# Second block of a two-block decoder trunk: x for the operands' sums comes in whole rows into the raw weights' places, the norm's diagonals are made ahead of their matmuls, and the weight sums begin with the first output units

## Chip, cores, metric

One Trainium2 chip, one core. The metric is the device time of one execution in microseconds (us); the time given for a kernel is the median of its runs. One execution is also taken by the hardware profiler; its records are the profile that is quoted here.

## What is computed

One layer of a decoder trunk on x of 2048 tokens by 1024 features, all in float32:

```
h = rmsnorm(x, mix_norm_g)
q, k, v, g, u = split(h @ w_in)                    # 4 x 512 columns for retention, 512 for pooling
y_ret  = silu(g) * head_rmsnorm(retention(rope(q), rope(k), v))
y_pool = pool_mixer(u)                             # trailing windows 2, 4, 8, 16
x = x + concat(y_ret, y_pool) @ w_out
x = x + cross_attn(rmsnorm(x), mem)                # 4 heads, 256 memory tokens
x = x + (silu(gate) * val) @ w_down                # gate, val: causal conv of width 3 over rmsnorm(x) @ w_up
out = rmsnorm(x)
```

## The kernel before

Features lie on the 128 partitions, tokens along the free dimension. The tokens are worked in **two blocks** of T = 1024 (b = 0, 1); in each, a stage works on halves of SUB = 512 tokens. A float32 product is made of three passes (`passes`, L266 to L268): every operand is split into a high half (fp32r, ScalarE) and a low half (the rest, VectorE), and high x high, high x low, low x high are summed in a PSUM bank (`mm`, five of them, beside two `aux` and one single). So each weight tile costs one ScalarE and one VectorE operation per 512 columns before TensorE can use it (`split`, `pairs`, and `high`, `low` of `Member`, L1092 and L242).

**Places.** SBUF is handed out by hand. `raws` are the places of unsplit weights: R (three of 128x1024) and two tiles S; `prs` are the places of split pairs, Q (three). `TT` is an arena of ten places T of 512 columns for everything short-lived. `Z` has eight places of 1024 columns. A place that is taken again makes its next writer wait for its last reader.

**Order.** The program is recorded in Python order, and a scheduler then sets each engine's order. Generators are advanced between products: `behind[0]` (work that must come soon: retention, norms), `under[0]` (the weight sums), and inside a stage one of its own. The order of an engine's queue, its SP queue of DMA issues included, is fixed once it is built; each waits for the instruction in front of it.

**Weight sums** (`weight_sums`). The second block's input projections and all of the gated MLP are done in seven products of half-size blocks instead of eight. They need sums of weight blocks, which GpSimd's DMA queue makes in DRAM: copies of 128x512 (L990) and accumulating transfers (L987). There are 42 jobs (8 for the head projections, 22 up, 12 down) of four steps each. One more job is begun at each step; a step starts with a halo copy on ScalarE (L1005) and one on GpSimd (L1006), behind which GpSimd issues up to eight transfers for the up to four jobs alive. `spacing[0]` calls of the generator lie between two steps. It is called after each quarter of a unit (while `slow[0]` holds, which is until the first block's output projection, after every second one), after each tile of the attention (L956; in the first block from its sixth on), after each quarter of the second block's values and after each of its 56 head products. In the products with VWd it is paused.

**The second block's start**, on which the change works. The last products of the first block (with VWd, `unit`) run beside the loading of the second block's x (`load_x`) and of the values' weights wv (`opening`, four loads into R and S). Then:

- `norms` (a generator in `behind[0]`) makes the factors of the norm by `rows_norm` (sums over partitions by TensorE, L347, then some 14 small VectorE operations) and spreads them over the partitions by `spread`: for each half a diagonal matrix per high and low part (VectorE, into a Q place), each followed at once by a matmul of `ones` with it (L371), and an evacuation (L376).
- `values` makes v: eight token tiles in four rounds of two banks, two half-rounds each; between them `between` advances `quarter_sums`, and the weight sums.
- `quarter_sums` makes the operands of the seven products from x, in four groups j. A group takes four T places, loads a quarter of 128x512 into each (L1540), and computes with ScalarE and VectorE the split of (x11 - x12) g1 into t1 (L1549, L1550), d3 and d4 into Z (L1555, L1559), and the negated split of x11 g1 + d3 into t2 (`negated`, L1562).
- `head_projections` turns `raws` into seven places of 512 columns (five in R, two in one S) and S0 into a fourth pair place, loads weights (`fetch`, L1086) and splits them up to four products ahead. Its first steps are `turned_sums` (d3 into t3 and d4 into the operand X) and `scaled_tables` (rope tables times the norm). It evacuates with L1659. One bank is summed on over several products, with an evacuation between them.

In the second attention (`attention`) ScalarE splits tables Md that SP loads (L905) among the first tiles' work, and the transposes of finished tiles (L920) stand among TensorE's products.

Of the kernel before, what the change touches and what calls it, by code (L numbers as in the profile page):

```python
# [8 lines left out]
F32 = mybir.dt.float32  # L9
F32R = mybir.dt.float32r  # L10
# [5 lines left out]
P = 128  # L16
# [120 lines left out]
def trunk(ctx, tc, xT, memT, pos, w_qkgu, w_v, wkv, wqT, wo, wout_r, wout_p, poolT, w_up, w_dn, vecs, consts, outT):  # L137
# [178 lines left out]
    def units(weights, rhs, evacs, order, at):  # L316
# [3 lines left out]
        for h in range(2):  # L320
            for hs, evac, banks in zip(weights, evacs, ps):
                if callable(hs[h]):
                    hs[h] = hs[h]()
                for s in range(NS):
# [4 lines left out]
                    quarter[0] += 1  # L329
                    if not slow[0] or quarter[0] % 2:  # L330
                        next(under[0], None)
# [23 lines left out]
    def spread(y, outs, keep=True, late=False):  # L355
# [8 lines left out]
        for out in outs:  # L364
# [12 lines left out]
            at += n  # L377
        return last

    def squares(k, src, s_ap, eng=dve):  # L380
# [316 lines left out]

    def values(rn, wp, step=lambda: None):
        v = Z.take(4)
        v4 = v.f.rearrange("p (h c d) -> p h c d", h=HEADS, c=KT)  # L700
# [191 lines left out]
    def attention(sums, beside, pace):  # L892
# [39 lines left out]
        for i in range(2 * KT):  # L932
# [631 lines left out]

    def head_projections(b, v, rb, tabs, t1, t2, z3, z4):

# [13 lines left out]
        def turned_sums():  # L1580
            for j in range(KT // 2):
                split(z3.f[:, j * SUB : (j + 1) * SUB], *fourth(t3, j))
                yield
            z3.free()
            for j in range(KT // 2):
                negated(z4.f[:, j * SUB : (j + 1) * SUB], *xpair(j, 1))
                yield
            z4.free()

# [285 lines left out]
    for b in range(NB):  # L1875
# [19 lines left out]
        else:  # L1895
            t1, t2 = (B.arenas[0].take(4) for _ in range(2))
            z3, z4 = Z.take(2), Z.take(2)
            more_sums = quarter_sums(b, t1, t2, z3, z4)

# [4 lines left out]

            v = values(lambda: normed[0], wv, between)
            for _ in more_sums:
# [4 lines left out]
            for i in range(2):  # L1911
                sp.dma_start(tabs[i].f[:, :SUB], rope_d[i])
            mix = head_projections(b, v, rb, tabs, t1, t2, z3, z4)
        for r in rb:
            r.free()
        slow[0], spacing[0] = False, (8, 4)[b]

# [43 lines left out]
        prob, behind[0] = attention(xs, beside, b + 1)  # L1961
        spacing[0] = 4
        for _ in beside:
# [56 lines left out]
        if b + 1 < NB:  # L2020
# [4 lines left out]
            def norms(xs, nxt, normed, own):  # L2025
# [134 lines left out]
```

## Time and profile before

| | us |
|---|---|
| median of 3 runs | 2492.06 |
| lowest, highest | 2489.83, 2493.7 |
| the profiled execution | 2488.75 |
| its span, first to last instruction | 2487.0 |
| mean granted TensorE clock | 0.991 |
| TensorE busy | 2424.5 |
| VectorE busy | 1731.5 |
| ScalarE busy | 1288.9 |
| GpSimd busy | 319.2 |

Names: PE is TensorE, DVE VectorE, ACT ScalarE, POOL GpSimd, SP SyncE, which issues most DMAs (SPq its queue). In a row of the order of time stand start, duration, engine, line, operation, out<-in, shape, and in brackets the idle time of the engine ahead of it and what ended it. In the chain of work stand start, duration and what was worked on or waited for. In the table of DMA issues stand out<-in, queue, count, KB each and the median time from issue to landing. L242, L250, L258 and L261 are helpers (two-input operations, fused three-input operations, and the two forms of a high half), so there the tiles tell what is meant.

### The profile page before, as it was taken

How to read it: one execution, taken by the hardware profiler on the slowest of the kernel's cores; microseconds unless marked ns; L12 is line 12 of the kernel's file. 1: busy time of each engine (PE TensorE's matmuls, PEld its weight loads, DVE VectorE, ACT ScalarE, POOL GpSimd, SP SyncE). 2: the span in 40 equal slices, each digit the busy share in tenths (PEclk: the TensorE clock that was granted, in tenths of full speed). 3: DMA queues.
4: the chain of work that ended last, by engine and by line, in shares of the span. 5: the costliest groups of instructions: out<-in, count | busy, mean ns of one | idle time of the engine just before them, and what ended most of it. 6: DMA issues, size and time to landing. Idle time of an engine off the chain costs nothing.

```text
span 2487.0 us, 33308 instructions
## 1 busy us (share of the span) xinstructions
PE 2424.5 (97%) x11294; PEld 2021.6 (81%) x11294; DVE 1731.5 (70%) x2921; ACT 1288.9 (52%) x2348; POOL 319.2 (13%) x485
## 2 busy tenths in 40 slices
PE   6999999999989999999999999999999999999997
PEld 6888888888777787788888888888888888888886
DVE  8645676565666666575588776797667688867875
ACT  6333423443334553334555555665555677666663
POOL 1002022031243424200000000020000000000000
PEclk9999999999999999999999999999999999999998
DMA  8245677677696959847458665665556468768951
GB/s 285 65 136 171 190 181 206 205 169 229 193 239 185 237 141 308 226 166 266 153 178 279 209 190 172 206 222 169 165 158 215 133 223 301 247 187 274 350 170 68
DMA packets 264315, 501.56 MB, mean 202 GB/s; under 512 B 28880, under 2 KB 57680, under 8 KB 264144
## 3 DMA queue, kind: packets, MB, share of 16 engines
q1 hardware_dynamic: 202256, 385.11, 47.6%
q0 software_dynamic: 37376, 86.00, 15.0%
q10 hardware_dynamic: 24512, 28.32, 3.3%
q8 instruction: 89, 1.46, 0.2%
q14 instruction: 82, 0.67, 0.1%
HBM read 398.13 MB, written 187.17 MB: 235 GB/s over the span
## 4 chain that ended last, share of the span: by engine, by line
PE 89%; DMA 4%; DVE 4%; ACT 2%; issue 1%; SPq 0%; POOLq 0%; POOL 0%; DVEq 0%; ACTq 0%
PE mm L266 28%; PE mm L267 28%; PE mm L268 28%; DMA T<-xT 1%; DVE T L242 1%; DMA T<-Xd 1%; PE aux L266 1%; PE aux L782 1%; PE aux L267 1%; PE aux L268 1%; PE aux L798 1%; PE aux L771 1%; DMA R<-Md 1%; PE aux L800 1%; DVE Z L242 0%
## 5 line engine op out<-in xcount | busy, mean ns | idle before, releaser
L266 PE MATMUL mm<-G,Q 128*128 128x512 f32 (+1 forms) x1745 | 675.6, 388 | 29.2 <-ACT Q L258 11.0
L268 PE MATMUL mm<-G,Q 128*128 128x512 f32 (+1 forms) x1745 | 671.0, 386 | 6.3 <-DVE Q L242 6.2
L267 PE MATMUL mm<-G,Q 128*128 128x512 f32 (+1 forms) x1617 | 622.1, 385 | 0.0
L267 PE MATMUL mm<-G,E 128*128 128x512 f32 x1084 | 421.6, 389 | 0.0
L266 PE MATMUL mm<-G,E 128*128 128x512 f32 x1084 | 420.0, 389 | 0.0
L268 PE MATMUL mm<-G,E 128*128 128x512 f32 x1084 | 419.2, 389 | 0.0
L266 PEld LDWEIGHTS mm<-G,Q 128*128 128x128 f32 x1745 | 332.8, 191 | 96.1 <-ACT Q L258 12.1
L268 PEld LDWEIGHTS mm<-G,Q 128*128 128x128 f32 x1745 | 332.1, 190 | 72.2 <-DVE Q L242 9.1
L267 PEld LDWEIGHTS mm<-G,Q 128*128 128x128 f32 x1617 | 308.9, 191 | 56.7
L242 DVE TENSOR_TENSOR Z<-Z,mm 128x512 f32<-128x512 f32 x296 | 202.1, 684 | 104.7 <-PE mm L268 104.4
L250 DVE SCALAR_TENSOR_TENSOR Z<-Z,vecs 128x1024 f32<-128x1024 f32 x176 | 224.8, 1281 | 50.4 <-ACT Z L1155 46.9
L268 PEld LDWEIGHTS mm<-G,E 128*128 128x128 f32 x1084 | 203.5, 188 | 42.4
L267 PEld LDWEIGHTS mm<-G,E 128*128 128x128 f32 x1084 | 203.5, 188 | 42.3
L266 PEld LDWEIGHTS mm<-G,E 128*128 128x128 f32 x1084 | 203.5, 188 | 42.0
L242 DVE TENSOR_TENSOR T<-T 128x512 f32<-128x512 f32 (+3 forms) x217 | 148.9, 689 | 39.5 <-ACT T L387 15.6
L1092 ACT ACTIVATE E<-R 128x512 fp32r<-128x512 f32 (+1 forms) x165 | 101.5, 615 | 143.0 <-PE mm L267 132.6
L242 DVE TENSOR_TENSOR G<-T,G 128x512 fp32r<-128x512 f32 (+1 forms) x185 | 122.6, 676 | 41.8 <-ACT G L1041 31.4
L242 DVE TENSOR_TENSOR Q<-R,Q 128x512 fp32r<-128x512 f32 x149 | 103.6, 698 | 65.1 <-ACT Q L258 46.0
L1092 ACT ACTIVATE Q<-R 128x512 fp32r<-128x512 f32 (+1 forms) x153 | 94.4, 617 | 88.0 <-PE mm L267 77.3
L1041 ACT ACTIVATE G<-T 128x512 fp32r<-128x512 f32 x160 | 97.7, 624 | 56.4 <-DMA T<-Hd 26.5
L1155 ACT ACTIVATE Z<-Z,vecs 128x1024 f32<-128x1024 f32 x88 | 109.2, 1242 | 33.3 <-DVE Z L242 32.4
L1092 ACT ACTIVATE E<-S 128x512 fp32r<-128x512 f32 (+1 forms) x107 | 65.8, 616 | 105.7 <-PE mm L267 104.4
(322 smaller groups left out, 3814.8 us busy)
## 6 DMA issues: line engine op xcount, KB each, us to landing
T<-Gd SPq DMA_DIRECT2D x173, 256.0 KB, 4.5
Ud<-w_up POOLq DMA_DIRECT2D x132, 256.0 KB, 9.2
Gd<-Z SPq DMA_DIRECT2D x110, 256.0 KB, 2.8
R<-Ud SPq DMA_DIRECT2D x106, 256.0 KB, 2.7
R<-w_up SPq DMA_DIRECT2D x80, 256.0 KB, 3.1
S<-Ud SPq DMA_DIRECT2D x70, 256.0 KB, 2.8
T<-xT SPq DMA_DIRECT2D x64, 256.0 KB, 4.9
Gd<-T SPq DMA_DIRECT2D x56, 256.0 KB, 3.3
```

Of the source, the lines that this page charges most:

```text
L242: return eng.tensor_tensor(out=out, in0=a, in1=b, op=op)
L250: dve.scalar_tensor_tensor(out=out, in0=a, scalar=s, in1=b, op0=op0, op1=op1)
L266: pe.matmul(ps, lh, rh, start=start, stop=False, skip_group_check=more)
L267: pe.matmul(ps, lh, rl, start=False, stop=False, skip_group_check=more)
L268: latest[0] = pe.matmul(ps, ll, rh, start=False, stop=stop, skip_group_check=more)
L771: pe.matmul(col(sc, c), self.ch(k, c), self.ch(q, c), start=True, stop=True)
L782: pe.matmul(col(self.kv, c), col(self.kn.f, c), self.ch(v, c, h * T), start=True, stop=True)
L798: pe.matmul(col(y, c), col(self.pr.f, c), self.ch(v, c, h * T), start=True, stop=self.cur[c] is None)
L800: pe.matmul(col(y, c), self.ch(q, c), self.cur[c], start=False, stop=True)
L1041: act.activation(hi, x, AF.Copy)
L1092: act.activation(p2[:, 0, :w], self.raw[i].f[:, :w], AF.Copy)
L1155: act.activation(self.c[g].f, a[:, 2:], AF.Identity, bias=cb[:, f : f + 1], scale=cw[2][:, f : f + 1])
```

## The change

Four things. **x in rows:** `quarter_sums` takes places of `raws` instead of T places: for a group two loads of 128x1024, x rows j and j + 4 of the block, each in a whole place of R or S; the first two groups are asked for ahead of the values, and group j + 2 when group j is done. One T place is left for a scratch. d3 and d4 lie in one Z region of four places that is taken with the values' region. **Diagonals ahead:** `spread_steps` makes all four diagonals (two pair places), waits two turns of the generator, and then issues the four matmuls and two evacuations. **Weight sums:** none in the first block's heads and pools; one call per quarter from the output units on with a spacing of 4 instead of 8; in the first attention from the third tile on instead of the sixth; a spacing of 3 instead of 4 in the second block's values and heads.

The diff's core (line numbers of after.py run 22 to 33 higher behind `spread_steps`):

```diff
@@ units
-                    if not slow[0] or quarter[0] % 2:
+                    if not slow[0]:
                         next(under[0], None)
@@ new, behind spread
+    def spread_steps(y, outs):
+        yh = smp.tile([P, 8], F32R, tag="yh", name=nm("yh"), bufs=1)[:, : y.shape[1]]
+        yl = small(y.shape[1])
+        dve.tensor_copy(yh, y)
+        tt(dve, yl, y, yh.bitcast(F32), ALU.subtract)
+        n, ds = SUB // P, []
+        for s in range(len(outs)):
+            ds.append(prs.take())
+            for i, v in enumerate((yh.bitcast(F32), yl)):
+                di = ds[s].r[:, i * SUB : (i + 1) * SUB]
+                tt(dve, di.rearrange("p (a b) -> p a b", a=n), ident..., bcast(v[:, s * n : (s + 1) * n], P), ALU.mult)
+        yield
+        yield
+        for out, d in zip(outs, ds):
+            ps = aux()
+            with tc.issue_after(latest[0].ins):
+                for i in range(2):
+                    pe.matmul(ps, ones, d.r[:, i * SUB : (i + 1) * SUB], start=i == 0, stop=i == 1)
+            d.free()
+            act.activation(out, ps, AF.Copy)
@@ attention
-            if pace > 1 or i > 4:
+            if pace > 1 or i > 1:
                 next(under[0], None)
@@ quarter_sums
+    def part_of(z, i, j):
+        at = (j // 2) * 2 * T + i * T + (j % 2) * SUB
+        return z.f[:, at : at + SUB]
+
-    def quarter_sums(b, t1, t2, z3, z4):
+    def quarter_sums(b, t1, t2, z):
+        def load(j):
+            out = []
+            for k in (j, j + 4):
+                out.append(new_raw())
+                sp.dma_start(out[-1], xT[k * P : (k + 1) * P, b * T : (b + 1) * T])
+            return [r[:, h * SUB : (h + 1) * SUB] for r in out for h in range(2)]
+
+        ahead = [load(0), load(1)]
+        yield
         for j in range(KT // 2):
-            x = [TT.take() for _ in range(4)]
-            for i, r in enumerate(x):
-                k, at = j + 4 * (i // 2), b * T + i % 2 * SUB
-                sp.dma_start(r.f[:, :SUB], xT[k * P : (k + 1) * P, at : at + SUB])
-            x11, x12, x21, x22 = (r.f[:, :SUB] for r in x)
-            d3, d4 = (z.f[:, j * SUB : (j + 1) * SUB] for z in (z3, z4))
+            x11, x12, x21, x22 = ahead.pop(0)
+            d3, d4 = part_of(z, 0, j), part_of(z, 1, j)
             g1, g2 = mixg[:, j : j + 1], mixg[:, j + 4 : j + 5]
-            yield
-            yield
-            x.append(TT.take())
-            t = x[4].f[:, :SUB]
+            r = TT.take()
+            t = r.f[:, :SUB]
             act.activation(t, x12, AF.Identity, scale=g1)
...
             stt(d4, x21, g2, x11, ALU.mult, ALU.subtract)
-            for r in x:
-                r.free()
+            r.free()
+            if j + 2 < KT // 2:
+                ahead.append(load(j + 2))
             yield
@@ trunk, second block
-            z3, z4 = Z.take(2), Z.take(2)
-            more_sums = quarter_sums(b, t1, t2, z3, z4)
+            v, z = Z.take(4), Z.take(4)
+            more_sums = quarter_sums(b, t1, t2, z)
+            next(more_sums)
...
-        slow[0], spacing[0] = False, (8, 4)[b]
+        slow[0], spacing[0] = False, (4, 4)[b]
...
         prob, behind[0] = attention(xs, beside, b + 1)
-        spacing[0] = 4
+        spacing[0] = 3
@@ norms
-                with tc.issue_after(latest[0].ins):
-                    normed[2] = spread(normed[0], [r.f[:, :SUB] for r in normed[1]], late=True)
-                yield
+                yield from spread_steps(normed[0], [r.f[:, :SUB] for r in normed[1]])
                 yield
```

What it does to the built order, at three places. The queue of **SP** at the second block's start, of before (T<-xT behind L1540 are the quarters for the sums, Ad and w_qkgu the head weights, R and S_79 the raw places):

```order
L1086 DMA R<-Ad 128x512
L1086 DMA R<-w_qkgu 128x512
L1540 DMA T<-xT 128x512
L1086 DMA R<-Ad 128x512
L1540 DMA T<-xT 128x512
L1086 DMA R<-Ad 128x512
L1086 DMA R<-w_qkgu 128x512 x2
L1086 DMA R<-Ad 128x512
L1540 DMA T<-xT 128x512
L1086 DMA R<-w_qkgu 128x512
L1540 DMA T<-xT 128x512 x10
L1086 DMA R<-Ad 128x512
```

And now (L1566 loads the x rows, L1108 the head weights; the first x row stands a few places earlier):

```order
L1566 DMA R<-xT 128x1024 x2
L1566 DMA S_78<-xT 128x1024
L1566 DMA R<-xT 128x1024
L1945 DMA T<-rope_d 128x512 x2
L1566 DMA R<-xT 128x1024
L1566 DMA S_79<-xT 128x1024
L1108 DMA R<-Ad 128x512
L1566 DMA R<-xT 128x1024
L1108 DMA S_79<-w_qkgu 128x512
L1108 DMA R<-Ad 128x512
L1108 DMA R<-w_qkgu 128x512
```

Eight of the head weights' loads stood ahead of nearly all of x; now none does, and x is through after eight loads.

The queue of **VectorE** around the norm's diagonals (Q<-consts,yh and Q<-consts,sm: their high and low parts), of before:

```order
L1791 COPY rn_5193<-sm_5204 128x8
L359 CAST yh_5240<-rn_5193 128x8
L242 TENSOR_TENSOR sm_5241<-rn_5193,yh_5240 128x8
L242 TENSOR_TENSOR Q<-consts,yh_5240 128x512
L242 TENSOR_TENSOR Q<-consts,sm_5241 128x512
L242 TENSOR_TENSOR T<-T 128x512
L250 SCALAR_TENSOR_TENSOR Z_4548<-T,vecs 128x512
L250 SCALAR_TENSOR_TENSOR T<-T,vecs,Z_4548 128x512
L250 SCALAR_TENSOR_TENSOR G<-T,vecs,G 128x512
L250 SCALAR_TENSOR_TENSOR Z_4548<-T,vecs 128x512
L250 SCALAR_TENSOR_TENSOR G<-T,G 128x512
L242 TENSOR_TENSOR Q<-consts,yh_5240 128x512
```

And now (R<-R is the first subtraction of the fourth group that is worked on, Z_4518<-S_79,vecs,T the third's d3):

```order
L242 TENSOR_TENSOR R<-R 128x512
L250 SCALAR_TENSOR_TENSOR sm_5188<-sm_5190,sm_5188 128x8
L1823 COPY rn_5177<-sm_5188 128x8
L384 CAST yh_5218<-rn_5177 128x8
L242 TENSOR_TENSOR sm_5219<-rn_5177,yh_5218 128x8
L242 TENSOR_TENSOR Q<-consts,yh_5218 128x512 x2
L250 SCALAR_TENSOR_TENSOR Z_4518<-S_79,vecs,T 128x512
L242 TENSOR_TENSOR Q<-consts,sm_5219 128x512 x2
L250 SCALAR_TENSOR_TENSOR G<-R,vecs,G 128x512
```

The second half's diagonals stood behind the six operations of one group's sums; now both halves' stand together, but all behind the sums of two groups (not in the rows) and one subtraction of a third. On TensorE the four matmuls with `ones` stood among the second round's products, two ahead of its second bank and two behind; now the first two stand behind the second bank's first half, the others six and eleven matmuls later.

The queue of **ScalarE** at the end of the values, of before (L711 evacuates the values, L1659 the head products, L1562 with L258 alternating are negations and the turned sums, L1092 the high halves of head weights):

```order
L1562 ACTIVATE G<-T 128x512
L1005 ACTIVATE halo<-consts 128x2
L711 ACTIVATE Z_4548<-mm_5374,rn_5193 128x4x128
L711 ACTIVATE Z_4548<-mm_5375,rn_5193 128x4x128
L1562 ACTIVATE G<-T 128x512
L1562 ACTIVATE G<-Z_4548 128x512
L258 ACTIVATE G<-Z_4548 128x512
```

And now (L733, L1592, L1114 and L400 are L711, L1562, L1092 and L376 of before):

```order
L1592 ACTIVATE G<-R 128x512
L400 ACTIVATE T<-aux_5275 128x512
L733 ACTIVATE Z_4518<-mm_5257,rn_5177 128x4x128
L1114 ACTIVATE Q<-R 128x512
L733 ACTIVATE Z_4518<-mm_5258,rn_5177 128x4x128
L1114 ACTIVATE S_5514<-R 128x512
L1114 ACTIVATE Q<-R 128x512 x2
L733 ACTIVATE Z_4518<-mm_5367,rn_5177 128x4x128
L733 ACTIVATE Z_4518<-mm_5368,rn_5177 128x4x128
L1027 ACTIVATE halo<-consts 128x2 x2
L1592 ACTIVATE G<-Z_4518 128x512
```

The last negation of a group (L1562 G<-T) stood behind the third round's evacuations, right ahead of the turned sums; now it stands ahead of the second round's, and four high halves of head weights, three of which stood ahead of all values' evacuations, stand between the evacuations of the second and the third round.

More of the change, by code (lines that the diff above doesn't have):

```diff
@@ L696, in value_weights, with values @@
         return u
-    def values(rn, wp, step=lambda: None):
-        v = Z.take(4)
+    def values(rn, wp, step=lambda: None, v=None):
+        v = v or Z.take(4)
         v4 = v.f.rearrange("p (h c d) -> p h c d", h=HEADS, c=KT)
@@ L1563, in negated, with head_projections @@
         stt(lo, src, -1.0, hi.bitcast(F32), ALU.mult, ALU.subtract)
-    def head_projections(b, v, rb, tabs, t1, t2, z3, z4):
+    def head_projections(b, v, rb, tabs, t1, t2, z):
         nonlocal raws, prs
@@ L1581, in turned_sums @@
             for j in range(KT // 2):
-                split(z3.f[:, j * SUB : (j + 1) * SUB], *fourth(t3, j))
+                split(part_of(z, 0, j), *fourth(t3, j))
                 yield
-            z3.free()
+            z.free(0, 1)
+            z.free(2, 1)
             for j in range(KT // 2):
-                negated(z4.f[:, j * SUB : (j + 1) * SUB], *xpair(j, 1))
+                negated(part_of(z, 1, j), *xpair(j, 1))
                 yield
-            z4.free()
+            z.free(1, 1)
+            z.free(3, 1)
         def scaled_tables():
@@ L1903, in between @@
                     next(under[0], None)
-            v = values(lambda: normed[0], wv, between)
+            values(lambda: normed[0], wv, between, v)
             for _ in more_sums:
@@ L1912, in trunk @@
                 sp.dma_start(tabs[i].f[:, :SUB], rope_d[i])
-            mix = head_projections(b, v, rb, tabs, t1, t2, z3, z4)
+            mix = head_projections(b, v, rb, tabs, t1, t2, z)
         for r in rb:
             r.free()
-        slow[0], spacing[0] = False, (8, 4)[b]
+        slow[0], spacing[0] = False, (4, 4)[b]
         xs = [TT.take() for _ in range(NS)]
```

1 line of the change is left out of this document (added).

## Prediction

> **What bounds the kernel now.** I read the page first, then the table of stretches, then TensorE's order of time for its holes, and last, for each hole, the chain of work that ended last.
>
> ```profile
> PE 2424.5 (97%) x11294; PEld 2021.6 (81%) x11294; DVE 1731.5 (70%) x2921; ACT 1288.9 (52%) x2348; POOL 319.2 (13%) x485
> PE 89%; DMA 4%; DVE 4%; ACT 2%; issue 1%; SPq 0%; POOLq 0%; POOL 0%; DVEq 0%; ACTq 0%
> ```
>
> And of the table of stretches (start and end in us, then busy time and instructions by engine, granted clock, DMA share, GB/s):
>
> ```profile
> core 0: us, PE busy (x) PEld busy (x) DVE busy (x) ACT busy (x) POOL busy (x), PEclk, DMA share, GB/s
> 657.00:708.00 51.00, 48.44 (x230) 40.32 (x229) 25.17 (x61) 15.28 (x27) 20.34 (x29) 1.00 0.86 225
> 708.00:772.00 64.00, 53.57 (x208) 42.08 (x208) 41.77 (x68) 26.49 (x49) 26.92 (x41) 0.89 0.84 215
> 772.00:940.00 168.00, 163.65 (x872) 137.60 (x871) 113.52 (x241) 84.62 (x220) 59.90 (x93) 1.00 0.74 187
> 940.00:1010.00 70.00, 67.97 (x296) 55.07 (x296) 40.95 (x68) 27.94 (x53) 29.11 (x48) 1.00 1.07 321
> 1010.00:1130.00 120.00, 115.35 (x535) 94.95 (x534) 76.00 (x172) 41.77 (x106) 9.78 (x15) 0.97 0.65 200
> ```
>
> TensorE is busy 97%, so the change has only holes to win: 2487.0 - 2424.5 = 62.5 us in the whole span, plus what slow restarts cost. Of the stretches, 708 to 772 (the head projections' first products) is the worst: over 10 us idle, and a granted clock of 0.89. The holes that the change can reach, with neighbours:
>
> ```profile
> 222.21 0.39 PE L266 MATMUL mm<-G 128*128 128x256 f32 x1 [2.37 <-ACT T L504]
> 680.44 0.49 PE L371 MATMUL aux<-Q,ones 128*128 128x512 f32 x1 [2.56 <-DVE Q L242]
> 680.78 0.39 PE L267 MATMUL mm<-E,G 128*128 128x512 f32 x1
> 681.00 0.40 PE L268 MATMUL mm<-E,G 128*128 128x512 f32 x1
> 715.98 0.39 PE L268 MATMUL mm<-G,S 128*128 128x512 f32 x1
> 721.02 0.79 PE L266 MATMUL mm<-G,Q 128*128 128x512 f32 x1 [4.66 <-ACT E L1659]
> 726.31 0.63 PE L266 MATMUL mm<-G,Q 128*128 128x512 f32 x1
> 726.74 0.46 PE L267 MATMUL mm<-G,Q 128*128 128x512 f32 x1
> 748.56 0.79 PE L266 MATMUL mm<-G,Q 128*128 128x512 f32 x1 [4.25 <-ACT Q L1092]
> 753.84 0.55 PE L267 MATMUL mm<-G,Q 128*128 128x512 f32 x1
> 1038.59 2.03 PE L920 MATMUL aux<-consts,T 128*128 128x128 f32 x8 [3.77 <-DVE T L246]
> 1043.84 0.61 PE L268 MATMUL mm<-G 128*128 128x512 f32 x1
> ```
>
> In rhythm, matmuls start 0.23 us apart (680.78, 681.00). After the hole of 2.56 us they do so at once; after those of 4.66, 4.25 and 3.77 us they start 0.43 us apart (726.31, 726.74) up to the later row of each pair, so nearly half of 4 to 6 us is lost too. Counted against the rhythm, the holes cost 2.4 (at 222), 2.8 (680), 4.66 + 0.4 + 14 x 0.2 = 7.9 (721), 4.25 + 0.2 + 13 x 0.2 = 7.1 (748) and 3.8 + 1.9 = 5.7 us (1038).
>
> [...]
>
> Who ended these holes, from the chain of work:
>
> ```profile
> 204.54 7.03 DMA R<-wo
> 661.88 13.06 DMA T<-xT
> 680.24 10.75 DMA T<-xT
> 704.03 8.31 DMA T<-xT
> 712.37 0.76 DVE Z L250
> 713.94 0.80 ACT G L1562 x2
> 718.83 1.14 ACT Z L711 x2
> 720.49 0.49 ACT E L1659
> 739.39 5.87 DMA R<-Ad
> 1016.04 13.55 DMA R<-Md
> ```
>
> Each begins with a slow DMA. 661.88, 680.24 and 704.03 are pieces of x, which wait for one of the ten T places. At 704 the last of them starts; VectorE's sum follows at 712.4, ScalarE's negation (L1562) at 713.9, and the evacuations L711 and L1659 stand behind it in ScalarE's queue: TensorE waits from 716.4 to 721.0. At 680 the norm's diagonals stand behind sums that wait for the 661.88 transfer. What makes transfers slow:
>
> ```profile
> T<-xT SPq DMA_DIRECT2D x4, 256.0 KB, 3.1
> T<-xT SPq DMA_DIRECT2D x3, 256.0 KB, 11.5
> Ud<-w_up POOLq DMA_DIRECT2D x6, 256.0 KB, 12.7
> S<-w_qkgu SPq DMA_DIRECT2D x9, 512.0 KB, 4.1
> L1005 ACT ACTIVATE halo<-consts x45: 184/188/258, 79.4 to 1038.5; 128x2 f32<-128x2 f32 x45
> ```
>
> The first row is of the window 640:656, without a burst of weight sums, the next two of 655:676, with one; the fourth is the whole span's. Each of the 45 halo copies lets POOL issue one step of weight sums, up to eight transfers of 256 KB, 2.1 MB.
>
> **The change part by part.**
>
> *Weight sums later.* Steps in block one: heads and pools 64 / 2 / 4 = 8 before, none now; outputs 32 / 8 = 4, now 32 / 4 = 8; attention 11 / 2, now 14 / 2 = 7. In block two: values and heads 72 / 4 = 18, now 72 / 3 = 24; outputs 8. So of 45 steps about 44 fell ahead of the second attention, the last at 1038.5; now 8 + 7 + 24 leave 6 for outputs that could hold 8 (in the built order only 3 copies stand there). Hence:
>
> (a) No burst meets the wo loads: 7.03 us falls towards 4.1, and 222's hole goes, **-2.4** (bounds 0 to -2.4).
>
> (b) The Md load of 1016.04, 13.55 us amid POOL's last steps, no longer meets them: at 8.5 us or less the norm and softmax behind it are 5 us earlier, and the hole of 3.77 goes with its restart, **-5.7** (0 to -5.7).
>
> (c) Block one's outputs get the burst rate that block two's bear: 940:1010 moves 321 GB/s at DMA share 1.07, and TensorE is idle 2.0 us of 70. Cost 0 to 2; the nearest row hides it, I take 0.
>
> (d) In the second heads a step comes each 8.2 us (3 products of 12 x 0.227 = 2.72) instead of 10.9, 5 more. 772:940 has DMA share 0.74 at 187 GB/s, so 253 GB/s fill it; 20 steps of 2.1 MB and 56 weight halves of 0.26 MB in 226 us are 251 GB/s: just full. Bounds: nothing (seven weight places are 7 x 2.72 = 19 us of lead, a load under a burst takes 6 to 12) or the 30 us of the slow rival below. I take **+4**: five more steps, each a hole under 1 us.
>
> *x rows in R and S.* Sixteen loads of 256 KB become eight of 512 KB that wait for no T place.
>
> ```profile
> 642.12 0.33 SPq L1086 DMA_DIRECT2D S<-w_qkgu  x1
> 655.77 2.79 SPq L1086 DMA_DIRECT2D R<-w_qkgu  x2
> 658.12 0.68 DVE L242 TENSOR_TENSOR Z<-Z,mm 128x512 f32<-128x512 f32 x1
> 679.70 0.69 DVE L242 TENSOR_TENSOR Q<-consts,yh 128x512 fp32r<-128x512 f32 x1
> 725.78 0.69 DVE L242 TENSOR_TENSOR Q<-R,Q 128x512 fp32r<-128x512 f32 x1
> ```
>
> The head weights of before (first two rows) show when S and R come free: five x rows can start from 642 to 656, ahead of the bursts. The other three wait for places that the first sums release. VectorE begins those right after its last residual (658.12), 13 operations of 0.6 to 0.75 us lie up to the release: 667. The load lands 4.1 us later at best, 13.06 at worst; I take twice the quiet 4.1, as a burst is then under way: 675.
>
> [...]
>
> *Diagonals ahead.* Both high diagonals now stand together behind the fourth group's first subtraction in VectorE's queue: 675 + 0.7 + 0.8 of small ones + 0.7 = 677, where the second pair was made at 679.70. TensorE comes to them near 677 (680.44 - 2.56 = 677.9, less two norm products that stood ahead). So a wait of 0 to 1 us; bounds 0 and, at 13.06, 5 to 6 us with 3 of slow restart. Behind the waiting matmul stand all the values' products. Nearest is the 2.8 of before: I book it as kept, **0**.
>
> *What is late next.* The first evacuations L711 now stand behind the fourth group's x in ScalarE's queue: done near 679, needed 36 matmuls (8.2 us) after the diagonals, near 686. Head weights load only when x leaves R: the last x row lands near 682, its five sums end at 686, a load of 8 and the split of 1.3 make 695; TensorE reaches them near 706 (before: 715.98 + 0.23 - 3 x 2.72 = 708). The turned sums wait for no x any more, only for the values' last first-half product, 24 x 0.227 ahead of the end: they start at 701, ScalarE is through at 706, and the first L1659 is done by 710; TensorE asks for it at 706 + 8.2 = 714. The hole at 721 goes, **-7.9** (bounds -4 to -7.9). VectorE's turned sums and rope scaling (16 operations) end at 712, where before its first low half came at 725.78: that is 7 us sooner against TensorE, and the Ad load of 739.39, which waits for a low half, moves as much. The hole at 748 goes, **-7.1** (0 to -7.1).
>
> Sum: -2.4 - 5.7 + 4 + 0 - 7.9 - 7.1 = -19.1. The profiled execution took 2488.75 us (span 2487.0) and becomes 2469.7; it lies 3.3 under the median of three, 2492.06, so the median becomes **2473**.
>
> **The rivals.** *The full queue outlasts the heads* (15%): in the values 6 steps of 2.1 MB and 4 MB of x are asked in 50 us, 330 GB/s of a 253 GB/s queue; POOL then lags by some 16 us, the heads at 251 give it no time to catch up, and it meets the Md load all the same. The 5.7 stay: 2479. Against it: only three steps are left for the outputs' 66 us.
>
> *The diagonals wait for a 13 us load* (13%): 6 + 3 us more at 677: 2482. For it: 661.88 and 680.24 both took over 10 us by a burst. [...]
>
> *The wait changes its place* (15%), so that the change does not do what it says: x keeps R and S so long that the first head weights come at 712 instead of 695 (two 13 us loads in series, then one under a burst): 6 us of hole and 2.8 of restart at the heads' start, on top of the diagonals' 9: 2491, no change.
>
> *Weights starve* (16%), slower: in the heads POOL's queue is never empty. If a weight load then takes 11.5 us or more and waits 7 for its place and in SP's order, the 19 us of lead are used up, and each of 20 bursts costs TensorE 1.5 us: 30 instead of 4, 2499. For it 708:772, where such a load is on the chain (739.39); against it 940:1010, full and nearly without holes.
>
> **How the numbers follow.** The forecast has 41%, at 2473. The range, 2461 to 2496, takes in the bounds (all gains whole, diagonals free, denser bursts free: 2466, and 5 for small holes that go along) and all cases up to the third rival, with 5 us above its middle; the starving of weights stays outside. About 0.2% (5 us) is what a measurement of this kernel can tell from no change. Faster: 41 + 15 + 13 and 2 of the third rival, 71%; same 15%, the rest of it and 2 of the last; slower 14%.
>
> **What would show it.** Holes at 222 and 1038 gone or not: the weight sums' place. The x rows' loads: 4 to 9 us, not 13. The aux matmuls near 677: idle under 3 us, and what ended it. The heads' fourth product: no idle, clock 1.00 from 708 to 772. TensorE's waits for ScalarE's Q in the heads: over 6 us in sum would be starving. I am wrong if a hole over 4 us stands at the heads' start, or if holes come in the rhythm of the bursts.

## The result and the profile after

The changed kernel takes **2482.44 us** (median of six runs, 2481.53 to 2485.51) against 2491.34 for the kernel before on the same chip: ratio 0.9966, interval 0.9953 to 0.9978. It is faster by 8.9 us, where 19 were forecast.

The page of the changed kernel, and its table of stretches (columns as above; the stretches are shifted with the work):

```profile
PE 2422.2 (98%) x11294; PEld 2020.2 (81%) x11294; DVE 1731.1 (70%) x2921; ACT 1289.8 (52%) x2348; POOL 318.8 (13%) x485
PE 91%; DMA 4%; DVE 3%; ACT 1%; issue 1%; SPq 0%; POOL 0%; POOLq 0%; ACTq 0%; DVEq 0%
```

```profile
470.00:500.00 30.00, 21.66 (x87) 17.41 (x86) 16.03 (x39) 7.58 (x14) 3.34 (x6) 0.83 0.74 232
665.00:716.00 51.00, 46.60 (x213) 38.70 (x212) 30.13 (x70) 18.80 (x37) 23.04 (x37) 0.93 0.95 270
716.00:780.00 64.00, 59.82 (x260) 48.61 (x259) 42.55 (x70) 26.95 (x48) 35.39 (x55) 0.97 1.06 272
780.00:943.00 163.00, 158.74 (x846) 133.38 (x845) 109.47 (x237) 82.55 (x220) 83.95 (x128) 1.00 0.95 237
943.00:1013.00 70.00, 67.97 (x297) 55.04 (x296) 41.02 (x67) 28.70 (x53) 23.54 (x36) 1.00 1.02 293
1013.00:1130.00 117.00, 115.19 (x547) 95.33 (x546) 75.56 (x171) 41.59 (x104) 0.00 (x0) 1.00 0.51 177
```

The second attention (last row) now has no GpSimd work and a clock of 1.00. The heads' first products (716 to 780) have lost most of their idle time. But 470 to 500, the end of the first block's outputs and the start of its attention, has become a bad stretch: TensorE busy 21.66 of 30 us, clock 0.83. Before the change it stood so:

```profile
470.00:500.00 30.00, 30.00 (x145) 25.05 (x144) 20.50 (x54) 11.42 (x25) 0.00 (x0) 1.00 0.45 150
```

TensorE's order of time in the changed kernel at the places that the prediction spoke of, and the new one:

```profile
218.75 0.39 PE L266 MATMUL mm<-G 128*128 128x256 f32 x1 [0.33 <-ACT T L526]
489.67 1.01 PE L347 MATMUL aux<-consts,T 128*128 128x1 f32 x4 [7.26 <-DVE T L242]
690.65 0.80 PE L398 MATMUL aux<-Q,ones 128*128 128x512 f32 x1 [4.40 <-DVE Q L242]
752.07 0.50 PE L266 MATMUL mm<-G,Q 128*128 128x512 f32 x1 [3.33 <-ACT Q L1114]
1037.62 1.03 PE L942 MATMUL aux<-consts,T 128*128 128x128 f32 x8
```

222's hole is down to 0.33 us, 1038's is gone, and so is 721's (no row). The hole at 748 has shrunk from 4.25 to 3.33 us, the one at the diagonals has grown from 2.56 to 4.40, and one of 7.26 us stands where none was.

Both kernels give TensorE the same 11294 instructions in nearly the same order, so the start of the k-th in one less the start of the k-th in the other is an account of where time goes:

| the k-th TensorE instruction | before | after | difference | since the row above | forecast there |
|---|---|---|---|---|---|
| 236 (opening) | 55.49 | 54.57 | -0.9 | -0.9 | 0 |
| 1152 (first block's heads) | 222.21 | 219.33 | -2.9 | **-2.0** | -2.4 |
| 2382 (end of its outputs) | 474.08 | 472.32 | -1.8 | +1.1 | 0 |
| 2487 (its attention) | 495.62 | 505.34 | +9.7 | **+11.5** | 0 |
| 3314 (values) | 674.01 | 684.63 | +10.6 | +0.9 | 0 |
| 3338 (behind the diagonals) | 681.71 | 694.83 | +13.1 | **+2.5** | 0 |
| 3540 (behind the hole at 721) | 736.26 | 740.87 | +4.6 | **-8.5** | -7.9 |
| 3587 (behind the hole at 748) | 754.23 | 756.86 | +2.6 | **-2.0** | -7.1 |
| 4530 (end of the heads) | 939.81 | 942.32 | +2.5 | -0.1 | +4 |
| 4960 (behind the hole at 1038) | 1044.52 | 1040.32 | -4.2 | **-6.7** | -5.7 |
| 11293 (the last) | 2476.37 | 2473.13 | -3.2 | +1.0 | 0 |

The account closes at 3 us, not at 9: the execution of before that was profiled took 2488.75 us, among the faster ones, and that of after 2485.51, the slowest of its six. The table is read for places, the medians for the total.

Who made the new hole, from the chain of work that ended last:

```profile
472.30 14.13 DMA S<-Md
486.45 0.64 ACT Z L258
487.11 1.29 DVE Z L242 x2
488.41 0.60 DVE G L242
489.01 0.61 DVE T L242
489.67 1.86 PE aux L347 x8
```

The attention's last Md load takes 14.13 us. ScalarE and then VectorE split it, and VectorE's part (Z) stands in its queue ahead of the outputs' last residual work (G and T), for which the norm's matmuls (L347) wait. It is the chain that the prediction told of at 1038, at the first block's attention instead of the second's. What slows the load, by the table of DMA issues in 472.0 to 472.5 of the changed kernel:

```profile
Ad<-w_qkgu POOLq DMA_DIRECT2D x2, 256.0 KB, 11.5
R<-Md SPq DMA_DIRECT2D x1, 512.0 KB, 12.3
S<-Md SPq DMA_DIRECT2D x1, 512.0 KB, 14.1
```

The outputs' eight steps are still being issued by GpSimd. **Theory:** the denser weight sums ahead of the first attention cost the 11.5 us; the bursts in the values cost the diagonals, and the load behind 752, the rest. **Rivals:** the attention's own earlier steps do it; the diagonals' new place does it; the denser heads do it.

### The profile page after: what moved, and what is told of

Read it like the earlier page. It is cut to its first block, busy times and chain, and to the rows that moved or that the text cites. A ratio compares the mean times of both kernels' runs of the same rounds, so it can differ in the third digit from the quotient of the medians.

```text
span 2483.7 us, 33285 instructions
## 1 busy us (share of the span) xinstructions
PE 2422.2 (98%) x11294; PEld 2020.2 (81%) x11294; DVE 1731.1 (70%) x2921; ACT 1289.8 (52%) x2348; POOL 318.8 (13%) x485
## 4 chain that ended last, share of the span: by engine, by line
PE 91%; DMA 4%; DVE 3%; ACT 1%; issue 1%; SPq 0%; POOL 0%; POOLq 0%; ACTq 0%; DVEq 0%
PE mm L266 28%; PE mm L267 28%; PE mm L268 28%; DMA T<-Xd 1%; DMA Z<-xT 1%; PE aux L793 1%; PE aux L804 1%; DMA S<-Md 1%; PE aux L820 1%; PE aux L266 1%; PE aux L267 1%; PE aux L268 1%; DVE Z L242 1%; PE aux L822 1%; DVE T L242 0%
## 5 line engine op out<-in xcount | busy, mean ns | idle before, releaser
L267 PE MATMUL mm<-G,Q 128*128 128x512 f32 (+1 forms) x1617 | 620.1, 384 | 0.0
L267 PE MATMUL mm<-G,E 128*128 128x512 f32 x1084 | 421.6, 389 | 0.0
L266 PEld LDWEIGHTS mm<-G,Q 128*128 128x128 f32 x1745 | 331.5, 190 | 89.5 <-ACT Q L258 11.5
L267 PEld LDWEIGHTS mm<-G,Q 128*128 128x128 f32 x1617 | 307.5, 190 | 56.3
L267 PEld LDWEIGHTS mm<-G,E 128*128 128x128 f32 x1084 | 203.5, 188 | 42.2
L1114 ACT ACTIVATE E<-R 128x512 fp32r<-128x512 f32 (+1 forms) x165 | 101.5, 615 | 142.0 <-PE mm L267 134.1
L1114 ACT ACTIVATE Q<-R 128x512 fp32r<-128x512 f32 (+1 forms) x153 | 94.5, 618 | 94.0 <-PE mm L267 75.0
L1114 ACT ACTIVATE E<-S 128x512 fp32r<-128x512 f32 (+1 forms) x107 | 65.9, 616 | 106.2 <-PE mm L267 102.7
```

The costliest lines, as they stand in the source:

```text
L266: pe.matmul(ps, lh, rh, start=start, stop=False, skip_group_check=more)
L267: pe.matmul(ps, lh, rl, start=False, stop=False, skip_group_check=more)
L1114: act.activation(p2[:, 0, :w], self.raw[i].f[:, :w], AF.Copy)
```

## The experiments

Times are medians, with the ratio to the kernel before in the same session and its interval. Three sessions ran on three chips, so between sessions the ratios are compared and not the times.

**The changed kernel again.**

> The changed kernel once more, as the anchor and for a second profile of it. Theory: 2481 to 2485 us, and the profile shows the same three places: TensorE idle for over 5 us at the first attention's start (7.3 us at 489.7 in the profile taken first) behind a load of Md of 12 us or more, 3 to 5 us at the diagonals (690), 3 us at the heads' fourth product (752). Rival: the hole at 489.7 was of that one execution (it was the slowest of six), then it is under 2 us here and the span some 8 us shorter than the median of six would say.

2482.84 us (five runs), 0.9967 (0.9954 to 0.9979), span of the profiled execution 2481.1. The hole at the attention's start stands at 488.59 with 5.6 us, the diagonals' at 688.1 with 3.8, the third at 749.2 with 3.2. The holes belong to the kernel, their sizes move by 1 to 2 us.

**Spacing 8 in the first outputs.**

```diff
-        slow[0], spacing[0] = False, (4, 4)[b]
+        slow[0], spacing[0] = False, (8, 4)[b]
```

> The changed kernel with the weight sums' spacing in the first block's output units put back from 4 to 8 (4 steps there instead of 8; the 4 others fall later, into the second block's output units). Theory: the eight steps fill GpSimd's DMA queue up to 486 us, so that the attention's last Md load (472.3, 14.1 us) is slow; with four the hole at 489.7 and its restart go, about 11 us: 2472. Rival 1: it is the attention's own earlier steps (from the third tile on) that slow the load: the hole stays, 2482. Rival 2: the four moved steps reach the second attention's Md load and bring back a hole near 1040: 2478.

2476.66 us, 0.9938 (0.9925 to 0.9951). The table of stretches and the DMA issues of 468.5 to 469.0 of this kernel:

```profile
470.00:500.00 30.00, 30.00 (x146) 25.02 (x145) 20.57 (x55) 12.12 (x29) 5.05 (x9) 1.00 0.51 150
```

```profile
S<-Md SPq DMA_DIRECT2D x1, 512.0 KB, 7.1
```

The last Md load takes 7.1 us, TensorE is never idle and the clock is 1.00, although the attention's own steps are still called from its third tile on: rival 1 is out. By the account against the changed kernel, TensorE is 11.6 us ahead behind this place. At the end 6.8 are left: the four moved steps widen the diagonals' hole (4.61), the heads' (3.70) and small ones up to 1032 in the second block. The 2472 expected was too good: steps that leave one place have to stand in another. The second rival's hole near 1040 is not there (0.60 us idle at most), though 1.6 us are lost around it.

**No steps in the last two first-block outputs.**

```diff
+            slow[0] = b == 0 and n >= 6
             unit(raw, mixed, add_residual(b, n, xs, got=got), (0, 2, 3, 1, 4, 6, 7, 5) if b == 0 else range(KT))
```

> The changed kernel, spacing 4 in the first output units kept, but no weight sums called in the last two of the eight units (6 steps instead of 8). Theory: GpSimd's queue is empty some 20 us before the attention's last Md loads, which then take 8 us or less instead of 14; the hole at 489.7 goes: 11 us under 2482.5, 2471.5. Rival: the rate fills the queue long before, so that the loads in the outputs themselves run late and the hole stays over 4 us: 2479.

2479.08 us, 0.9948 (0.9935 to 0.9960). The hole at 489 is gone here too (S<-Md 6.9 us), so it is the queue's tail at the Md loads that costs, not the rate in the outputs. But in the second block the steps now reach the same chain, and TensorE waits at its attention's start:

```profile
1000.52 11.98 DMA S<-Md
1012.52 0.64 ACT Z L258
```

```profile
1015.74 1.27 PE L347 MATMUL aux<-consts,T 128*128 128x1 f32 x6 [3.91 <-DVE T L242]
```

From 14.6 us ahead of the changed kernel in the heads, this one is 6.9 ahead behind that place: the hole takes back 7.7, with a slow restart (the six narrow matmuls behind it take 1.27 us, where six take 0.81 at 673.81 in the kernel with the steps put where nothing waits), which the expectation had not counted. The time is that of its rival (2479), the cause is not.

**The x rows alone** (the kernel before, with `quarter_sums` and its callers as changed).

> The kernel before with the x rows in R and S alone: old schedule of weight sums, old making of the diagonals. Theory: the holes at 721 and 748 give 8.5 and 2 us, as in the changed kernel, and the diagonals cost 0 to 2.5 more: 8 to 10 under before, 2482. Rival: without the moved bursts the x rows land as late as the quarters did, and the gain is under 3: 2489.

2479.77 us, 0.9956 (0.9943 to 0.9968): 12.2 us faster than before, some 3 us more than the whole change, with intervals that overlap. 721's hole is gone, the one of 748 is 3.13 us, the diagonals' 1.68. The second attention's hole (4.53) and 222's (1.83) stay, as they must with the old schedule.

**The schedule alone** (the kernel before, with the four edits of the weight sums' calls).

> The kernel before with the schedule of weight sums alone. Theory: 222's hole gives 2.2, the second attention's 6.7, the first attention's start costs 11.5: 2 to 3 over before, 2494. Rival: the schedule carries the whole gain and the x rows nothing: 2482.

2498.66 us, 1.0031 (1.0018 to 1.0043): **slower** than before by 6.7. The expected terms are there, and in TensorE's order of time another that I had not expected:

```profile
731.87 0.80 PE L266 MATMUL mm<-G,Q 128*128 128x512 f32 x1 [8.12 <-ACT E L1659]
762.02 0.80 PE L266 MATMUL mm<-G,Q 128*128 128x512 f32 x1 [5.88 <-ACT Q L1092]
```

Where the x still comes in quarters that wait for T places, the denser steps in the values make the two heads' holes larger (4.66 and 4.25 before). So the parts do not add: -12.2 and +6.7 make -5.5, the whole makes -9, and the diagonals ahead, which are in neither part, do not bring the rest (see the next experiment). With the x rows asked for ahead, the denser values do no harm at 721 (-8.5 in the account above).

**Diagonals the old way, spacing 8** (`spread` in place of `spread_steps`).

```diff
-                yield from spread_steps(normed[0], [r.f[:, :SUB] for r in normed[1]])
+                with tc.issue_after(latest[0].ins):
+                    normed[2] = spread(normed[0], [r.f[:, :SUB] for r in normed[1]], late=True)
+                yield
                 yield
```

> Spacing 8 in the first output units, and the diagonals made as in the kernel before (a half's diagonal, its matmul, then the other half's). Theory: making all four diagonals at once puts them behind the fourth group's x row; made the old way the hole at the diagonals is the 1.7 us of the run with the x rows alone, instead of 4.6 and its half-clock restart: 4 us under the 2476.7 of the same kernel with the diagonals ahead, 2473. Rival: it is the bursts of the denser schedule that slow that x row, and the diagonals wait for it in either order: the hole stays over 4 us, 2477.

2474.88 us, 0.9936 (0.9924 to 0.9949). The hole is 3.35 us instead of 4.61. The time is 1.8 us lower, but on a chip where the kernel before is 1.5 lower too; the ratios are 0.9936 and 0.9938. Whether making the diagonals together costs something stays open. Three quarters of the wait are there in either order, and behind them stands the x row: ScalarE idles 9.14 us for it up to 676.04, and VectorE makes the first diagonal at 678.10, behind the subtraction that follows.

**No weight sums called in the values, spacing 8.**

```diff
-                if next(more_sums, None) is None:
-                    next(under[0], None)
+                next(more_sums, None)
```

> Spacing 8 in the first output units, diagonals ahead, and no weight sums called in the values' rounds (they begin with the head products, so that some steps move later). Theory: the fourth group's x row lands in 4 to 5 us instead of 8 to 9 and TensorE waits under 1 us for the diagonals: 5 us less there; the moved steps cost 0 to 2 at the end: 2473. Rival: the row starts too late in any case (it waits for a place), the hole stays over 2.5 us: 2476.

2481.83 us, 0.9965 (0.9953 to 0.9978): slower than with them (2476.66), but the place behaved as the theory has it. In TensorE's order of time there is no wait for the diagonals, and the heads' hole has gone as well:

```profile
730.50 0.50 PE L266 MATMUL mm<-G,Q 128*128 128x512 f32 x1 [0.54 <-ACT Q L1114]
```

In the heads this kernel is 13.8 us ahead of the one with steps there. All of it and more is lost in the second attention (by the account 13.6 us ahead at 1016, 1.8 behind at 1130), into which the last steps fall: the halo copies of this kernel (first and last start behind the colon), and of the changed one:

```profile
L1027 ACT ACTIVATE halo<-consts x45: 186/188/258, 378.5 to 1092.7; 128x2 f32<-128x2 f32 x45
```

```profile
L1027 ACT ACTIVATE halo<-consts x45: 186/188/255, 378.2 to 976.1; 128x2 f32<-128x2 f32 x45
```

**Spacing 4 in the second block's values and heads, spacing 8 in the outputs.**

> Spacing 8 in the first output units and 4 instead of 3 in the second block's values and heads. Theory now: the denser steps cost nothing in the heads, so they gain nothing here (772 to 940 the same within 1 us), but some eight steps fall into the second attention and bring back the hole at its first transposes (near 1031), 4 to 6 us: 2482. By the term of the prediction (4 us for spacing 3) the heads would be 4 us shorter: 2477.

2486.49 us, 0.9981 (0.9972 to 0.9990). The heads' hole at their start is 2 us smaller with fewer steps around it (1.77 us idle for 3.70); from there to 1016 TensorE gains nothing on the kernel with 3 (it loses 1.1), so the denser steps cost nothing in the heads' run. The spilled steps meet loads in the second attention, later and at a higher price than expected (9.4 us by the account, where 4 to 6 were counted):

```profile
1102.78 1.08 PE L942 MATMUL aux<-consts,T 128*128 128x128 f32 x4 [6.71 <-DVE T L246]
```

**Spacing 2 there.**

> Spacing 8 in the first output units, and 2 instead of 3 in the second block's values and heads: a step of 2.1 MB each 5.4 us, with the weights 480 GB/s where 253 were the most that was seen there. Theory: at 3 the heads lose nothing because the queue of GpSimd may lag, and the weights' loads keep 6 to 9 us and a lead of 19; at 2 the queue lags further but the loads hardly slow, so TensorE's holes from 772 to 940 grow by under 3 us; the values' burst is denser, so the diagonals' hole grows by 0 to 4: 2478. Rival (the prediction's starving): loads pass 11.5 us and every burst costs 1.5 us: over 2495.

2479.72 us, 0.9948 (0.9936 to 0.9961). The stretch 780 to 930 with spacing 4, 3 and 2 (all with spacing 8 in the first outputs):

```profile
780.00:930.00 150.00, 145.92 (x763) 121.89 (x762) 101.15 (x218) 77.25 (x204) 54.25 (x85) 1.00 0.76 197
```

```profile
780.00:930.00 150.00, 146.23 (x779) 122.89 (x778) 99.99 (x219) 77.10 (x212) 75.43 (x121) 1.00 0.95 243
```

```profile
780.00:930.00 150.00, 146.85 (x769) 122.87 (x767) 102.44 (x221) 77.89 (x211) 90.43 (x144) 1.00 1.08 281
```

The 253 GB/s of the expectation were worked out from a share; these rows are what the stretch moved. From 197 to 281 GB/s TensorE's busy time does not fall. The loads of Ad in the same stretch, again with 4, 3 and 2:

```profile
R<-Ad SPq DMA_DIRECT2D x10, 256.0 KB, 5.3
```

```profile
R<-Ad SPq DMA_DIRECT2D x10, 256.0 KB, 6.8
```

```profile
R<-Ad SPq DMA_DIRECT2D x10, 256.0 KB, 6.7
```

In these stretches GpSimd issued 76, 107 and 128 transfers of 192 or 256 KB: from 107 on, more of them do not slow the loads. The step to 2 does cost 4.5 us by the account at the outputs' start (2.67 us idle at 949.18, with matmuls 0.43 us apart behind it, for 0.76 at 950.64). Weights do not starve.

**Begun after the 24th quarter.** The old making of the diagonals, nothing called in the values and the first twelve head products, spacing 8 in the first and 3 in the second block's outputs, and:

```diff
-                    if not slow[0]:
+                    if not slow[0] or quarter[0] > 24:
```

> A version that follows the experiments: x rows in R and S, diagonals made the old way, the weight sums begun in the first block's last heads and pools (after the 24th quarter, spacing 4), spacing 8 in its output units, none in the values and the first twelve head products, then 3. Theory: no hole at 222 and 489 (no burst meets the loads behind them), the diagonals' hole under 2 us, the head products' hole (3.3 us at 752) under 1 as the load behind it takes 3 us instead of 6: 2466. Rival: the pool bursts open holes of their own, or the head hole stays as its load is asked for too late in any case: 2472.

2481.38 us, 0.9966 (0.9953 to 0.9978): the rival's cause, 9 us above its time. 222, 489, 680 and 752 are free, but the steps each four quarters open two other holes, at 264.79 (3.22 us) and 348.28 (4.51 us), with slow restarts: behind the first, matmuls start 0.43 us apart up to 270.7; behind the second, seven of L804 take 1.86 us, where eight take 0.89 at 312.19. The second, from TensorE's order of time and the chain:

```profile
348.28 1.01 PE L804 MATMUL aux<-Z,T 128*128 128x128 f32 x3 [4.51 <-ACT T L799]
```

```profile
332.78 13.08 DMA WPd<-T
345.95 0.60 ACT T L565
```

A store of a folded weight takes 13.08 us amid the steps, and ScalarE waits for it ahead of the work that TensorE needs.

**Steps put where nothing waits.** Six steps in the first block's heads and pools at the old rate, spacing 8 in its outputs, none called in the values, 3 in the heads and in the second outputs:

```diff
-                    if not slow[0]:
+                    if not slow[0] or quarter[0] % 2 and not 16 < quarter[0] <= 32:
-        slow[0], spacing[0] = False, (4, 4)[b]
+        slow[0], spacing[0] = False, (8, 3)[b]
-                if next(more_sums, None) is None:
-                    next(under[0], None)
+                next(more_sums, None)
```

> x rows and diagonals ahead as in the changed kernel; the weight sums: in the first block's heads and pools as in the kernel before except for quarters 17 to 32 (where the step of 201 us met the wo load), spacing 8 in its output units, none called in the values, 3 in the heads, 3 in the second block's output units. Theory: all steps are through before the second attention, no hole over 2 us at 222, 489, 680 and 752: 13 us under the 2476.7 of the kernel with spacing 8 in the outputs, 2464. Rival: the steps in the first block's heads open holes as they did when begun after the 24th quarter (9 us at 265 and 348): 2473.

**2468.63 us**, 0.9904 (0.9889 to 0.9919): 24 us under the kernel before and, by the ratios, some 15 under the changed one. ScalarE's rows around the heads' hole, of the changed kernel and of this one:

```profile
740.39 0.63 ACT L1114 ACTIVATE Q<-R 128x512 fp32r<-128x512 f32 x1 [1.60 <-PE mm L267]
748.88 0.63 ACT L1114 ACTIVATE S<-R 128x512 fp32r<-128x512 f32 x1 [5.10 <-DMA R<-Ad]
```

```profile
721.85 0.63 ACT L1114 ACTIVATE Q<-R 128x512 fp32r<-128x512 f32 x1 [1.60 <-PE mm L267]
726.81 0.63 ACT L1114 ACTIVATE S<-R 128x512 fp32r<-128x512 f32 x1 [1.57 <-DMA R<-Ad]
```

The load behind the second row of each, by the DMA issues, 742 to 743 of the changed kernel and 723.9 to 724.2 of this one:

```profile
R<-Ad SPq DMA_DIRECT2D x1, 256.0 KB, 6.2
```

```profile
R<-Ad SPq DMA_DIRECT2D x1, 256.0 KB, 2.7
```

3.5 us less for the load, 3.5 us less idle on ScalarE, 2.8 less on TensorE (0.54 for 3.33). Likewise the fourth group's x row, the one that the diagonals stand behind:

```profile
R<-xT SPq DMA_DIRECT2D x1, 512.0 KB, 8.6
```

```profile
R<-xT SPq DMA_DIRECT2D x1, 512.0 KB, 4.1
```

It is 4.5 us shorter, and the hole of 4.40 is gone. By the account this kernel stays 13.6 us ahead of the one with spacing 8 up to the start of the second attention, as expected. There 4.7 are lost, about as much as the 4.6 that the time lies above the one expected: TensorE idles 2.1 us at 1006, behind an Md load of 9.45 us, among the norm's narrow matmuls (128x1), and the matmuls behind start 0.43 us apart up to 1012.

**The same with the old diagonals.**

> The same with the diagonals made as in the kernel before. Theory: with no burst in the values the x row is in time and the diagonals' place decides nothing: within 2 us of the kernel with them ahead. Rival: the diagonals ahead are worth 2 to 4 us where x is in time: 2467.

2470.24 us, 0.9911 (0.9897 to 0.9924). No wait at the diagonals in either, and by the account both gain 2.8 us on the kernel before from the end of the first attention to behind the diagonals; 1.6 us apart, and the profile of this one has 5.2 us at 1008 instead of 2.1, in a stretch that the edit does not touch. Where x is in time, making the diagonals ahead is worth nothing that shows.

## Why the prediction was wrong

The sign was right; of the 19 us forecast 8.9 came, less than half. The time (2482.4) lies inside the range, but by a cost at a place that none of its cases named, and that the second rival has 2482 is chance: its 9 us at the diagonals were 2.5. By the prediction's own steps:

- **(a) 222 and (b) 1038 held**: -2.0 for -2.4, -6.7 for -5.7, for the reason given: the wo load takes 3.57 us instead of 7.03, the Md load 4.0 instead of 13.55. With the old schedule (the x rows alone) both holes stay, and that Md load takes 15.07.
- **(c) failed, and it is the main one.** "Block one's outputs get the burst rate that block two's bear ... Cost 0 to 2; the nearest row hides it, I take 0." It cost 11.5 us in the profiled execution and 9.0 in the second profile. The row that was to hide it, 940:1010, spoke for loads within the outputs, and these are indeed hidden but for 1.1 us. What it could not speak for is what comes behind: the queue's tail meets the attention's Md loads. Step (b) priced that chain for the second block, and the prediction did not ask where the first block's eight steps would end. Two kernels that empty the queue before the loads show it: S<-Md 7.1 and 6.9 us, no hole.
- **721 held**: -8.5 for -7.9. The first evacuations do not stand behind x any more.
- **748 was mis-sized**: -2.0 for -7.1. "The Ad load of 739.39, which waits for a low half, moves as much" was wrong. The high half that ScalarE makes ahead of that low half and the low half itself, of before, and the low half of the changed kernel (its high half, 740.39, is shown above):

```profile
734.95 0.63 ACT L1092 ACTIVATE Q<-R 128x512 fp32r<-128x512 f32 x1 [1.60 <-PE mm L267]
738.68 0.68 DVE L242 TENSOR_TENSOR Q<-R,Q 128x512 fp32r<-128x512 f32 x1
```

```profile
741.82 0.69 DVE L242 TENSOR_TENSOR Q<-R,Q 128x512 fp32r<-128x512 f32 x1
```

  Before, the low half started 3.7 us behind the high half, as VectorE was late; now it starts 1.4 behind. The high half waits in both kernels for TensorE to free a pair place (1.60 <-PE mm L267), and an earlier start of VectorE cannot move that: of the 7 us 2.3 were won against TensorE, and no more than 3.1 could be (3.7 less the 0.63 of the high half). The rest is the load's 6.2 us: where it takes 2.7, in the kernel with the steps put where nothing waits, the place gives -6.4.
- **The diagonals** were booked at 0 and cost 2.5 more, between the forecast and the second rival. The row was expected to start at 667 and land at 675; it started at 679.21 (with TensorE 10 us late, 669), as the first sums waited for an x row of 5.92 us, and took 8.58 where I had 8. The hole of 4.40 us then had a slow restart: matmuls 0.43 us apart up to 694.83, granted clock 0.50.
- **(d) heads, +4, was too dear**: -0.1. The sum "251 of 253 GB/s: just full" spread 20 steps over 226 us, which at 8.2 us each last 164, and took the 253 from a share. The changed kernel's heads moved 237, and spacing 2 moved 281 in the stretch without harm there. The fourth rival, starving, has nothing for it.

The first rival had the right kind of cause, a full queue that outlasts its stage, but put it at the heads. Of the prediction's signs, the x rows' loads (5.9 and 8.6 us, no 13) and the holes at 222 and 1038 came as it said; the idle time at the heads' fourth product (3.33 us) and at the diagonals (4.40) did not. Of the gains, 2.0 + 8.5 + 2.0 + 6.7 = 19.2 came in where 23.1 were forecast; of the costs, 11.5 + 2.5 = 14.0 where 4 were. The remaining +2.0 of the account are the small rows that no step had.

How long a hole must be for a slow restart, the runs do not show. In the kernel before, 2.56 us at 680 was followed by the rhythm of 0.23 us and 3.77 us at 1038 by matmuls 0.43 us apart; between these two the holes do not sort by length. After 3.13 us (x rows alone, 739) and 3.23 (old diagonals with spacing 8, 739) the granted clock stays at 1.00. After 2.67 us (spacing 2, 949) it falls to 0.50; after 3.22 (begun after the 24th quarter, 265) matmuls start 0.43 us apart, and after 3.33 (the changed kernel, 752) the clock is 0.50 from 753.7 to 756.2. Length alone does not decide; what else does stays open.

A 256 KB load of the head weights takes 2.7 us where no packet moves as it is issued (723.9 to 724.2, steps put where nothing waits), and at the median of ten 5.3 beside 76 of GpSimd's transfers in 150 us, 6.8 beside 107 and 6.7 beside 128: from 107 on, more work in the other queue does not lengthen it further, which goes against the starving rival. Twice the quiet 4.1 us, the prediction's estimate for a 512 KB load beside a burst, fits the 8.58 of the x row. The 12.3 and 14.1 us of the Md loads lie well above it, with other loads of SP in flight beside them; whether these or GpSimd's transfers make the difference, no run here separates.

## What to carry to other kernels

Work in the background can cost next to nothing in the stage that bears it (1.1 us in the first block's outputs here), and have its price at the stage's end (11.5 us), where the queue's tail meets the next stage's first loads: follow each moved transfer to where the queue runs empty, not only to where it is issued. Ask of each wait which load in it takes 6 to 14 us (6.2, 8.6 and 14.1 in the changed kernel) where a quiet one takes 3 to 4 (2.7 and 4.1 in the kernel with the steps put where nothing waits), and move the background away from those few loads instead of thinning it everywhere. Background work that is taken out of one place must be counted into another, and the version that did so by place gained 24 us where the change gained 9.

## What the hardware showed that was not expected

- A head weight's load of 256 KB kept its 6.7 to 6.8 us when the traffic in the stretch rose from 243 to 281 GB/s (5.3 at 197): with more of GpSimd's transfers beside it, it did not get slower.
- The 253 GB/s that the prediction took for all that fits were passed by 28 with TensorE's busy time in the stretch unchanged (281 GB/s, 146.85 of 150 us; 146.23 at 243).
- A hole of 2.67 us (spacing 2, 949) was followed by matmuls 0.43 us apart at a granted clock of 0.50, one of 3.23 us (old diagonals with spacing 8, 739) left the clock at 1.00.
- One kernel's executions differ by up to 8 us (2470.2 to 2478.7 in the five of spacing 8), another's by 2.3 (2466.9 to 2469.2). That the first has more waits that hang on transfers may be the reason, but it is not shown: the kernel without steps in the last two outputs has such waits too, and its five differ by 1.7.
